# A streaming encoder step on TensorE: 1092 token columns in blocks of 512, 512 and 68 in place of three of 364

## The chip, the cores and the metric

The kernel runs on one core of a Trainium2 chip. The metric is the device time of one execution in microseconds (us); smaller is better. The core has TensorE (PE, matrix products, with its weight loads shown apart as PEld), VectorE (DVE), ScalarE (ACT), GpSimd (POOL) and SyncE (SP, here the queue of the weight transfers).

## The reference

A two-layer encoder trunk takes one inference step for two groups that share all weights: 1024 frames of a new stream and 64 frames of a running one. All sizes below are float32.

```
x = x + mixer_l(rmsnorm(x)); x = x + conv_ffn(rmsnorm(x))          # l = 0, 1; then a last rmsnorm
layer 0's mixer: proj = h @ ab_w_in (1024 x 5648); a Mamba-2 scan and a gated short convolution;
                 concat(1024, 1024) @ ab_w_out
layer 1's mixer: proj = h @ lru_w_in (1024 x 2048); convolution, gates (4 heads, 256 x 256), linear scan;
                 (gelu(gate) * hs) @ lru_w_out
conv_ffn:        g, u = h @ ffn_w_in (1024 x 5632); (gelu(conv3(g)) * u) @ ffn_w_out (2816 x 1024)
```

The outputs are the final frames and the new states of the convolutions and scans.

## The kernel before, in words

Activations lie transposed: a tile is [128 features, T token columns], T = 1092: 1024 frames of the new stream, 4 columns of padding, 64 frames of the running one. D = 1024 features are 8 such tiles (KT).

Nearly all the arithmetic is in large products of weights with these tiles. To keep float32's precision, each operand is split into two parts of type float32r, a high part h and a rest l; `weights` (lines 122 to 134) loads 128 x 512 weights from HBM through SP's queue, ScalarE rounds them to wh (line 131) and VectorE makes the rest wl (line 132). A product is then wh with xh, wl with xh and wh with xl.

`product` (lines 160 to 169) fills one PSUM tile: for every 128-row tile of the contraction and each of the three pairs, it walks over the NB = 3 blocks of BL = 364 columns. A PSUM tile (`psum`, [128, 3, 512]) has three banks of 512 columns, and each block of 364 begins at the first column of its own bank. Two such tiles are in turn. Each matmul on TensorE is preceded by a load of its 128 x 128 weights, also where the weights are those of the matmul before.

Three routines call it. `project` (lines 176 to 182) makes one tile of an input projection, 8 x 3 x 3 = 72 matmuls. `chunk` (lines 255 to 262) adds two k-tiles of an output projection to the 8 residual tiles, 18 matmuls each, and VectorE adds the PSUM tile to the residual at line 260. `part` inside `gates` makes the RG-LRU gates. The results are read from PSUM as [128, 3, 364] by VectorE (lines 260, 608, 615 and others) or ScalarE; `b3` (lines 49 to 51) gives an SBUF tile the same three-block view. dt's product at line 327 has weights of only 48 columns (w_dt).

In layer 0 the small float32 products of the scan (lines 376, 465, 480, 507, 518, 520) are generators in the list `between`; `tick` lets one advance after each k-tile of a large product, so they stand in TensorE's queue between the large matmuls. Line 520 multiplies the state st, 128 columns of weights, by 64 columns; line 480 has 128 columns; lines 376 and 465 are transposes. The program's order on each engine is then set by a scheduler when the program is built. Norms (`rms`, line 210) and the last output product (`finish`, lines 743 to 758) have their own loops over blocks of 364. The final norm at line 758 is a plain float32 product with a matrix of ones.

Of the kernel before, what the change touches and what calls it, by code (L numbers as in the profile page):

```python
# [14 lines left out]
D = 1024  # L15
# [15 lines left out]
def columns():  # L31
    """Where each small parameter stands in the packed array of them."""
    at, n = {}, 0
    for k in ("mix0", "mix1", "fn0", "fn1", "fin", "ssdn"):
        at[k] = n
        n += KT
    for k, (c, w) in CONVS.items():
        at[k + "_w"], at[k + "_b"], at[k + "_h"] = n, n + c * w, n + c * (w + 1)
        n += c * (2 * w)
    for k, c in (("ba", 8), ("bx", 8), ("lam", 8), ("st", 8), ("dsk", 8), ("dtb", 1), ("alog", 1)):  # L40
        at[k] = n
        n += c
    return at, n
# [5 lines left out]
def b3(t):  # L49
    """A [128, T] tile seen as its token blocks."""  # L50
    return t[:, 0:T].rearrange("p (b n) -> p b n", b=NB)


def program(nc, tc, a, ctx):
# [44 lines left out]

    # ---- constants and small parameters  # L100
    par = const.tile([P, NPAR], F, name="par")
# [18 lines left out]

    # ---- helpers
    def weights(src):
        """A [128, 1024] tile of weights as its halves' parts (h, l), h + l the weights."""
        out = []
        for i in range(2):
            n = n_of["w"] = n_of.get("w", 0) + 1
            raw = wp.tile([P, 512], F, tag="raw", bufs=3, name=f"raw{n}")
            h = wp.tile([P, 512], R, tag="wh", bufs=6, name=f"wh{n}")
            l = wp.tile([P, 512], R, tag="wl", bufs=6, name=f"wl{n}")
            nc.sync.dma_start(raw, src[:, i * 512:(i + 1) * 512])  # L130
            S.activation(h, raw, AF.Copy)  # L131
            V.tensor_sub(l, raw, h.bitcast(F))  # L132
            out.append((h, l))
        return out

    def piece(w, j):
        """The j-th 128 columns of a tile of weights."""
        at = slice(j % 4 * P, (j % 4 + 1) * P)
        return w[j // 4][0][:, at], w[j // 4][1][:, at]

    # small products and what follows from them, made between the parts of the large ones
    between, ticks = [], {"n": 0}
# [17 lines left out]
    def product(ps, terms):  # L160
        """ps[m, t] = the sum over terms ((wh, wl) [k, m], (xh, xl) [k, t])."""
        n = len(terms) * 3
        i = 0
        for (wh, wl), (xh, xl) in terms:
            for w, x in ((wh, xh), (wl, xh), (wh, xl)):
                for b in range(NB):
                    TE.matmul(ps[:, b, 0:BL], w, x[:, b * BL:(b + 1) * BL], start=i == 0, stop=i == n - 1)  # L167
                i += 1
            tick()
# [6 lines left out]
    def project(key, xs):  # L176
        if key not in ahead:
            prefetch(key)
        w = ahead.pop(key)
        ps = psum()  # L180
        product(ps, [(piece(w, k), xs[k]) for k in range(KT)])
        return ps[:, :, 0:BL]

# [20 lines left out]
    def rms(ss, width):  # L204
        """ss [128, T] becomes 1/sqrt(mean + eps) of its sums over the partitions, in every row."""
        v, r, out = wk(), wk(), ss
        for b in range(NB):
            at = slice(b * BL, (b + 1) * BL)
            ps = aux().rearrange("p a b -> p (a b)")[:, 0:BL]
            TE.matmul(ps, ones, ss[:, at], start=True, stop=True)  # L210
            rstd(ps, v[:, at], r[:, at], out[:, at], width)
        return out

    def rstd(sums, v, r, out, width):
        """1/sqrt(sums/width + eps): by the table, then a step of Newton's."""
        S.activation(r, sums, AF.Abs_reciprocal_sqrt, bias=eps, scale=1.0 / width)
        V.tensor_scalar(v, sums, 1.0 / width, EPS, op0=OP.mult, op1=OP.add)
        S.activation(out, r, AF.Square)
        V.scalar_tensor_tensor(out, out, -0.5, v, op0=OP.mult, op1=OP.mult)
        V.scalar_tensor_tensor(out, out, 1.5, r, op0=OP.add, op1=OP.mult)  # L220

    def history(cb, kind, i):
        """The conv buffer's columns in front of each sequence."""
        n = CONVS[kind][1] - 1
        G.memset(cb[:, 0:PAD], 0.0)
        G.tensor_copy(cb[:, PAD + S0 - n:PAD + S0], col(kind + "_h", i * n, n))  # L226
# [11 lines left out]
    def softplus(x, tmp1, tmp2):  # L238
        """In place; x may be any AP."""
        S.activation(tmp1, x, AF.Abs)  # L240
        V.tensor_scalar_min(tmp1, tmp1, 80.0)
        S.activation(tmp2, tmp1, AF.Exp, scale=-1.0)
        # e^-|x|, corrected by what its logarithm is off
        ln = softplus.ln
        S.activation(ln, tmp2, AF.Ln)
        V.tensor_add(tmp1, tmp1, ln)
        V.tensor_scalar(tmp1, tmp1, -1.0, 1.0, op0=OP.mult, op1=OP.add)
        V.tensor_mul(tmp2, tmp2, tmp1)
        V.tensor_scalar_add(tmp1, tmp2, 1.0)
        S.activation(ln, tmp1, AF.Ln)  # L250
        V.scalar_tensor_tensor(tmp1, tmp1, -1.0, tmp2, op0=OP.add, op1=OP.subtract)
        V.tensor_sub(ln, ln, tmp1)
        V.scalar_tensor_tensor(x, x, 0.0, ln, op0=OP.max, op1=OP.add)

    def chunk(xs, ws, XR, done=None):
        """XR[m] += the product of the k-tiles xs with their rows of the output weights."""
        for m in range(KT):
            ps = psum()
            product(ps, [(piece(w, m), x) for w, x in zip(ws, xs)])
            V.tensor_add(b3(XR[m]), b3(XR[m]), ps[:, :, 0:BL])  # L260
            if done:
                done(m)

    class Next:
        """The norm that follows a residual sum: its operands and row of 1/rms."""

# [14 lines left out]
    def chunks(n, produce, w_out, XR, done, after):  # L281
        """The output product over n k-tiles, two at a time, one tile behind their making."""
        tiles = {}
# [17 lines left out]

    # ---- layer 0's mixer: the norm of x
    w_in = "ab_in"
    xin, XGs = [], []
    for k in range(KT):
# [4 lines left out]
        if k == 0:  # L310
            # dt's weights: their h for the rows from 0 and their l for those from 32
            raw_dt = wp.tile([P, 512], F, tag="raw", bufs=3, name="raw_dt")[:, 0:3 * H * KT].rearrange("p (k n) -> p k n", k=KT)
# [11 lines left out]
    for k in range(KT):  # L324
        for i in range(2):
            for b in range(NB):
                TE.matmul(ps[0:3 * H, b, 0:BL], w_dt[:, k], XGs[k][i][:, b * BL:(b + 1) * BL], start=k + i == 0, stop=k + i == KT)  # L327
    dt16 = ring()
    S.activation(b3(dt16)[0:H], ps[0:H, :, 0:BL], AF.Copy)
    V.tensor_add(b3(dt16)[0:H], b3(dt16)[0:H], ps[32:32 + H, :, 0:BL])  # L330
    raw_z = wk()
# [4 lines left out]

    # dt, the running sums of dt * A in each chunk, and what follows from them
    at_d = scratch("at_d", [H, T])
# [25 lines left out]
    nc.gpsimd.dma_start(cd, al_d.partition_broadcast(P))  # L364
    # the same by token: [token of the chunk, chunk, head]
    at_t = small([P, NCH + 1, H], "at_t")
# [20 lines left out]
    def silu_conv(i, ps, make):  # L387
        """The tile i of x, B or C: scaled, through its conv and SiLU."""
        cb = conv_buffer()
# [39 lines left out]
    def heads(i, xs, zz):  # L429
        """The scan of heads 2i and 2i+1; xs and zz are [head, p] by token."""  # L430
        h0 = 2 * i
# [15 lines left out]

        # the masked decays from token to token
        for h, Rt in ((h0, Ra), (h0 + 1, Rb)):
# [7 lines left out]
        S.activation(Re, Re, AF.Exp)  # L457
        # x * dt by token, and that decayed to the chunk's end
        Xd, Xe = ring(cols=L), ring(cols=L)
# [13 lines left out]
        yield  # L473
        # the chunks' states
        Hs = ring(cols=L)
# [22 lines left out]
        yield  # L498
        # y: within the chunk, D * x, and from the state at its start
        for q in range(3):  # L500
# [75 lines left out]

    # both halves' output product
    XR, RS2 = [], {}
# [46 lines left out]

    # ---- layer 1's mixer
    XGs = nxt.xs
# [38 lines left out]
    def gates(hd, xb, sx, nx):  # L666
        ax = weights(a["lru_ax"][hd])

        def part(o):
            ps = psum()  # L670
            product(ps, [(piece(ax, 4 * k + o), sx[k]) for k in range(2)])
            return ps[:, :, 0:BL]

# [54 lines left out]
    def finish(xs, ws):  # L728
        """The last part of the output product, the final norm and y, by blocks of tokens."""
        ss = slot("ss", 2)  # L730
# [62 lines left out]

# ---- layouts
def tiles_of(w):
    """[1024, m * 128] weights as m tiles [128, k * 128]: [k in the tile, (k tile, m in the tile)]."""
    m = w.shape[1] // P
# [3 lines left out]
def by_partition(v):  # L801
    """(..., c * 128) -> [128, c, ...]."""
    v = np.asarray(v)
# [105 lines left out]
```

## Time and profile before

| what | us |
|---|---|
| median of two runs | 2793.74 (2792.61 to 2794.87) |
| span of the profiled execution, first to last instruction | 2790.8 |
| TensorE busy: matmuls, weight loads | 2745.5, 2717.2 |
| VectorE, ScalarE, GpSimd busy | 1601.7, 803.4, 242.8 |

The page lists no time of the profiled execution beyond its span. The median is 2.9 us above that. Matmuls are pipelined: a recorded duration holds the way through the array, so two in a row overlap, and the pace of a stretch is the distance of starts. The granted clock is TensorE's: 1.00 is 2.4 GHz, 0.50 is 1.2 GHz.

### The profile page before, as it was taken

The numbers are of one execution on the slowest core, as the hardware profiler recorded it, in microseconds if no ns is written. First come the engines' busy times: TensorE is split into PE (matmuls) and PEld (weight loads), VectorE is DVE, ScalarE is ACT, GpSimd is POOL, SyncE is SP. The second block draws the span as 40 slices with busy tenths as digits, with TensorE's granted clock in tenths as the row PEclk, the third lists the DMA queues.
The fourth block names the chain that finished last, engine by engine and source line by source line (L and its number), as shares of the span: only waits on it lengthen the run. The fifth ranks groups of instructions, "written<-read, shape, count | busy, mean of one in ns | idle before, by whom it ended". The sixth has DMA issues, their size and how long they took to land.

```text
span 2790.8 us, 39161 instructions
## 1 busy us (share of the span) xinstructions
PE 2745.5 (98%) x16642; PEld 2717.2 (97%) x16642; DVE 1601.7 (57%) x1723; ACT 803.4 (29%) x1083; POOL 242.8 (9%) x524
## 2 busy tenths in 40 slices
PE   8999999999999999999999999999999999999998
PEld 8999999999989999999999989999899999999997
DVE  7655665568675444444444587786744444444446
ACT  7323322232132222212212245551412112212223
POOL 1101111010030000000000030020300000000003
PEclk9999999999999999999999999999999999999999
DMA  3222332244211111111111121151111111111111
GB/s 131 78 82 81 99 97 82 86 127 138 66 43 41 46 46 46 42 46 42 46 46 45 64 82 58 55 199 53 38 46 46 42 46 45 42 46 42 42 47 68
DMA packets 83103, 183.02 MB, mean 66 GB/s; under 512 B 9808, under 2 KB 12416, under 8 KB 82928
## 3 DMA queue, kind: packets, MB, share of 16 engines
q1 hardware_dynamic: 67248, 123.40, 14.5%
q0 software_dynamic: 15392, 56.69, 6.1%
q8 instruction: 131, 2.15, 0.3%
q10 hardware_dynamic: 288, 0.42, 0.0%
q14 instruction: 44, 0.36, 0.0%
HBM read 156.81 MB, written 23.66 MB: 65 GB/s over the span
## 4 chain that ended last, share of the span: by engine, by line
PE 94%; DVE 3%; issue 1%; ACT 1%; DMA 0%; POOL 0%; SPq 0%; DVEq 0%; ACTq 0%; POOLq 0%
PE pm L167 90%; DVE xg L193 1%; PE pa L507 1%; DVE xr L260 1%; PE pa L480 1%; PE pm L743 1%; DVE xg L772 0%; PE pa L518 0%; DVE wl L132 0%; PE pm L327 0%; PE pa L210 0%; PE pa L465 0%; DMA xr<-x 0%; DMA o_keep_lru<-keep_lru 0%; ACT xg L747 0%
## 5 line engine op out<-in xcount | busy, mean ns | idle before, releaser
L167 PE MATMUL pm<-xg,wh 128*128 128x364 f32 x7104 | 1406.8, 330 | 0.0
L167 PEld LDWEIGHTS pm<-xg,wh 128*128 128x128 f32 x7104 | 1204.6, 188 | 5.8 <-issue 2.6
L167 PE MATMUL pm<-xg,wl 128*128 128x364 f32 x3552 | 783.7, 328 | 0.0
L131 ACT ACTIVATE wh<-raw 128x512 fp32r<-128x512 f32 x440 | 274.8, 628 | 1481.7 <-PE pm L167 1259.8
L167 PE MATMUL pm<-ring,wh 128*128 128x364 f32 x3360 | 662.6, 331 | 22.3 <-DVE xr L260 17.2
L167 PEld LDWEIGHTS pm<-xg,wl 128*128 128x128 f32 x3552 | 619.9, 188 | 1.1
L167 PEld LDWEIGHTS pm<-ring,wh 128*128 128x128 f32 x3360 | 573.5, 189 | 27.4 <-DVE xr L260 20.2
L260 DVE TENSOR_TENSOR xr<-xr,pm 128x1092 f32<-128x1092 f32 x264 | 340.2, 1290 | 210.2 <-PE pm L167 204.4
L132 DVE TENSOR_TENSOR wl<-raw,wh 128x512 fp32r<-128x512 f32 x440 | 310.5, 708 | 243.8 <-ACT wh L131 243.6
L167 PE MATMUL pm<-ring,wl 128*128 128x364 f32 x1680 | 373.7, 331 | 0.0
L167 PEld LDWEIGHTS pm<-ring,wl 128*128 128x128 f32 x1680 | 295.4, 189 | 0.1
L226 POOL COPY wk<-par 128x2 f32<-128x2 f32 (+1 forms) x72 | 40.0, 555 | 1709.8 <-DVE wk L608 1416.2
L236 DVE SCALAR_TENSOR_TENSOR wk<-wk,par,wk 128x1092 f32<-128x1092 f32 x104 | 140.8, 1354 | 63.3 <-ACT wk L234 61.8
L608 DVE TENSOR_TENSOR wk<-pm,ss 128x1092 f32<-128x1092 f32 x44 | 57.0, 1295 | 193.0 <-PE pm L167 192.8
L615 DVE TENSOR_TENSOR wk<-pm,wk 128x1092 f32<-128x1092 f32 x44 | 57.0, 1295 | 119.7 <-PE pm L167 119.7
L187 DVE TENSOR_TENSOR ring<-wk,ring 128x1092 fp32r<-128x1092 f32 x68 | 87.9, 1294 | 36.5 <-ACT ring L186 32.8
L186 ACT ACTIVATE ring<-wk 128x1092 fp32r<-128x1092 f32 x68 | 75.7, 1116 | 100.0 <-PE pm L167 65.4
L612 DVE TENSOR_TENSOR wk<-wk,ss 128x1092 f32<-128x1092 f32 x44 | 57.0, 1296 | 52.1 <-ACT wk L611 52.1
L234 ACT ACTIVATE wk<-wk,par 128x1092 f32<-128x1092 f32 x52 | 67.7, 1302 | 65.5 <-POOL wk L226 65.3
L611 ACT ACTIVATE wk<-wk 128x1092 f32<-128x1092 f32 x44 | 49.2, 1118 | 121.2 <-DVE wk L236 121.2
L202 POOL TENSOR_TENSOR ss<-ss,wk 128x1092 f32<-128x1092 f32 x21 | 64.7, 3082 | 172.5 <-ACT wk L201 172.0
L193 DVE SCALAR_TENSOR_TENSOR xg<-xr,par,xg 128x1092 fp32r<-128x1092 f32 x32 | 64.5, 2024 | 11.8 <-ACT xg L192 11.5
(239 smaller groups left out, 1326.4 us busy)
## 6 DMA issues: line engine op xcount, KB each, us to landing
raw<-f_in SPq DMA_DIRECT2D x176, 256.0 KB, 2.6
raw<-ab_in SPq DMA_DIRECT2D x88, 256.0 KB, 2.7
raw<-f_out SPq DMA_DIRECT2D x88, 256.0 KB, 2.6
ring<-at_d POOLq DMA_DIRECT2D x16, 546.0 KB, 6.0
raw<-ab_out SPq DMA_DIRECT2D x32, 256.0 KB, 2.7
raw<-lru_in SPq DMA_DIRECT2D x32, 256.0 KB, 2.6
xr<-x SPq DMA_DIRECT2D x8, 546.0 KB, 7.3
ring<-at_d POOLq DMA_DIRECT2D x16, 273.0 KB, 7.9
```

The lines of the kernel that those rows point to most:

```text
L131: S.activation(h, raw, AF.Copy)
L132: V.tensor_sub(l, raw, h.bitcast(F))
L167: TE.matmul(ps[:, b, 0:BL], w, x[:, b * BL:(b + 1) * BL], start=i == 0, stop=i == n - 1)
L186: S.activation(h, src, AF.Copy)
L187: V.tensor_sub(l, src, h.bitcast(F))
L193: split_last[0] = V.scalar_tensor_tensor(l, src, scale, h.bitcast(F), op0=OP.mult, op1=OP.subtract).ins
L202: by.tensor_add(ss, ss, sq)
L234: S.activation(out, cb[:, at:at + T], AF.Identity, bias=col(kind + "_b", i), scale=col(kind + "_w", i * w))
L236: V.scalar_tensor_tensor(out, cb[:, at + k:at + k + T], col(kind + "_w", i * w + k), out, op0=OP.mult, op1=OP.add)
L260: V.tensor_add(b3(XR[m]), b3(XR[m]), ps[:, :, 0:BL])
L608: V.tensor_mul(b3(cb[:, PAD:]), ps, b3(RS))
L612: V.tensor_mul(g, g, RS)
```

## The change

The 1092 columns of a large product are cut at multiples of 512, so the PSUM tile is filled as one row of 1092 columns across its three banks: 512 columns in the first, 512 in the second, 68 in the third. `flat` gives that view and is used wherever such a tile is read; `b3` becomes the plain [128, 1092] view. The dt product at line 327 is cut in the same way. The loops of `rms` and `finish` stay at 364. Comments and document strings are left out in the changed file, so lines shift by up to ten: 167 becomes 177, 520 becomes 530.

```diff
 def b3(t):
-    return t[:, 0:T].rearrange("p (b n) -> p b n", b=NB)
+    return t[:, 0:T]
+
+BANK = 512
+BLOCKS = [slice(c, min(c + BANK, T)) for c in range(0, T, BANK)]
+
+def flat(ps):
+    return ps.rearrange("p b n -> p (b n)")[:, 0:T]
...
     def product(ps, terms):
...
             for w, x in ((wh, xh), (wl, xh), (wh, xl)):
-                for b in range(NB):
-                    TE.matmul(ps[:, b, 0:BL], w, x[:, b * BL:(b + 1) * BL], start=i == 0, stop=i == n - 1)
+                for at in BLOCKS:
+                    TE.matmul(flat(ps)[:, at], w, x[:, at], start=i == 0, stop=i == n - 1)
...
     def project(key, xs):
...
-        return ps[:, :, 0:BL]
+        return flat(ps)
...
     def chunk(xs, ws, XR, done=None):
...
-            V.tensor_add(b3(XR[m]), b3(XR[m]), ps[:, :, 0:BL])
+            V.tensor_add(b3(XR[m]), b3(XR[m]), flat(ps))
...
     ps = psum()
     for k in range(KT):
         for i in range(2):
-            for b in range(NB):
-                TE.matmul(ps[0:3 * H, b, 0:BL], w_dt[:, k], XGs[k][i][:, b * BL:(b + 1) * BL], start=k + i == 0, stop=k + i == KT)
+            for at in BLOCKS:
+                TE.matmul(flat(ps)[0:3 * H, at], w_dt[:, k], XGs[k][i][:, at], start=k + i == 0, stop=k + i == KT)
     dt16 = ring()
-    S.activation(b3(dt16)[0:H], ps[0:H, :, 0:BL], AF.Copy)
-    V.tensor_add(b3(dt16)[0:H], b3(dt16)[0:H], ps[32:32 + H, :, 0:BL])
+    S.activation(b3(dt16)[0:H], flat(ps)[0:H], AF.Copy)
+    V.tensor_add(b3(dt16)[0:H], b3(dt16)[0:H], flat(ps)[32:32 + H])
...
         def part(o):
...
-            return ps[:, :, 0:BL]
+            return flat(ps)
```

TensorE's queue in layer 0, at the end of one projection (PSUM tile pm_1219), a small product of the scan (line 520, into pa) and the start of the next projection (pm_1326); xg are parts of the normed input, wh and wl parts of the weights. Before:

```order
L167 MATMUL pm_1219<-xg_152,wh_1214 128x364 x3
L167 MATMUL pm_1219<-xg_152,wl_1215 128x364 x3
L167 MATMUL pm_1219<-xg_153,wh_1214 128x364 x3
L520 MATMUL pa_1307<-xr_563,st_769 128x64
L167 MATMUL pm_1326<-xg_93,wh_1315 128x364 x3
L167 MATMUL pm_1326<-xg_93,wl_1316 128x364 x3
```

The same place in the changed kernel:

```order
L177 MATMUL pm_1219<-xg_152,wh_1214 128x512 x2
L177 MATMUL pm_1219<-xg_152,wh_1214 128x68
L177 MATMUL pm_1219<-xg_152,wl_1215 128x512 x2
L177 MATMUL pm_1219<-xg_152,wl_1215 128x68
L177 MATMUL pm_1219<-xg_153,wh_1214 128x512 x2
L177 MATMUL pm_1219<-xg_153,wh_1214 128x68
L530 MATMUL pa_1307<-xr_563,st_769 128x64
L177 MATMUL pm_1326<-xg_93,wh_1315 128x512 x2
L177 MATMUL pm_1326<-xg_93,wh_1315 128x68
L177 MATMUL pm_1326<-xg_93,wl_1316 128x512 x2
L177 MATMUL pm_1326<-xg_93,wl_1316 128x68
```

The products keep their places; each row of three blocks becomes a row of two and a row of one, and the last of each three, before the weights change, is now the short one. In the feed-forward part the same queue reads as follows at the end of a piece of the output product (pm_10740, from the parts ring of the hidden tiles) and the start of the next projection (pm_10772). Before:

```order
L167 MATMUL pm_10740<-ring_10384,wh_10595 128x364 x3
L167 MATMUL pm_10740<-ring_10384,wl_10596 128x364 x3
L167 MATMUL pm_10740<-ring_10385,wh_10595 128x364 x3
L167 MATMUL pm_10772<-xg_7005,wh_10761 128x364 x3
L167 MATMUL pm_10772<-xg_7005,wl_10762 128x364 x3
```

After:

```order
L177 MATMUL pm_10740<-ring_10384,wh_10595 128x512 x2
L177 MATMUL pm_10740<-ring_10384,wh_10595 128x68
L177 MATMUL pm_10740<-ring_10384,wl_10596 128x512 x2
L177 MATMUL pm_10740<-ring_10384,wl_10596 128x68
L177 MATMUL pm_10740<-ring_10385,wh_10595 128x512 x2
L177 MATMUL pm_10740<-ring_10385,wh_10595 128x68
L177 MATMUL pm_10772<-xg_7005,wh_10761 128x512 x2
L177 MATMUL pm_10772<-xg_7005,wh_10761 128x68
L177 MATMUL pm_10772<-xg_7005,wl_10762 128x512 x2
```

Here too nothing but the cut of each three differs. SP's queue has the same order in both kernels; on VectorE, ScalarE and GpSimd some neighbouring instructions change places.

## Rows read from the trace of the kernel before

**Rows 1.** The page: span, busy time of each engine, granted clock in 40 slices
```profile
span 2790.8 us, 39161 instructions
...
PE 2745.5 (98%) x16642; PEld 2717.2 (97%) x16642; DVE 1601.7 (57%) x1723; ACT 803.4 (29%) x1083; POOL 242.8 (9%) x524
...
PEclk9999999999999999999999999999999999999999
```

**Rows 2.** The chain that ended last: by line, and its two longest pieces
```profile
PE pm L167 90%; DVE xg L193 1%; PE pa L507 1%; DVE xr L260 1%; PE pa L480 1%; PE pm L743 1%; DVE xg L772 0%; PE pa L518 0%; DVE wl L132 0%; PE pm L327 0%; PE pa L210 0%; PE pa L465 0%; DMA xr<-x 0%; DMA o_keep_lru<-keep_lru 0%; ACT xg L747 0%
...
837.19 762.97 PE pm L167 x4585
...
1993.04 753.60 PE pm L167 x4523
```

**Rows 3.** Groups of line 167 (busy us, mean ns of one | idle before)
```profile
L167 PE MATMUL pm<-xg,wh 128*128 128x364 f32 x7104 | 1406.8, 330 | 0.0
L167 PEld LDWEIGHTS pm<-xg,wh 128*128 128x128 f32 x7104 | 1204.6, 188 | 5.8 <-issue 2.6
L167 PE MATMUL pm<-xg,wl 128*128 128x364 f32 x3552 | 783.7, 328 | 0.0
...
L167 PE MATMUL pm<-ring,wh 128*128 128x364 f32 x3360 | 662.6, 331 | 22.3 <-DVE xr L260 17.2
...
L167 PE MATMUL pm<-ring,wl 128*128 128x364 f32 x1680 | 373.7, 331 | 0.0
```

**Rows 4.** Timeline, feed-forward of layer 0 (start us, us in all, engine, line)
```profile
1100.59 1.02 PEld L167 LDWEIGHTS pm<-xg,wh 128*128 128x128 f32 x6
1100.75 1.16 PE L167 MATMUL pm<-xg,wh 128*128 128x364 f32 x6
```

**Rows 5.** Timeline of PE from 1619.4 us, at granted clock 0.50
```profile
1620.37 2.02 PE L167 MATMUL pm<-ring,wh 128*128 128x364 f32 x6
1622.18 1.11 PE L167 MATMUL pm<-ring,wl 128*128 128x364 f32 x3
```

**Rows 6.** The stretch of rows 5: us, busy us of PE, PEld, DVE, ACT, POOL; PEclk, DMA share, GB/s
```profile
1618.00:1622.00 4.00, 3.62 (x12) 3.62 (x13) 3.18 (x4) 3.64 (x4) 2.39 (x3) 0.50 0.53 212
```

**Rows 7.** The final norm's float32 products: timeline of PE, and the line's durations
```profile
2772.06 5.06 PE L758 MATMUL pa<-xg,ones 128*128 128x364 f32 x16
...
L758 PE MATMUL pa<-xg,ones x16: 469/469/469, 2772.1 to 2776.6; 128*128 128x364 f32 x16
```

**Rows 8.** Line 327's weight loads, 48 columns (ns min/median/max, first and last start)
```profile
L327 PEld LDWEIGHTS pm<-xg,w_dt x48: 120/121/201, 9.0 to 24.8; 128*48 128x48 f32 x48
```

**Rows 9.** Timeline around line 520, from 141.36 us
```profile
141.16 0.32 PE L167 MATMUL pm<-xg,wh 128*128 128x364 f32 x1
141.32 0.33 PE L520 MATMUL pa<-xr,st 128*128 128x64 f32 x2
141.33 0.19 PEld L520 LDWEIGHTS pa<-xr,st 128*128 128x128 f32 x1
141.44 0.30 PEld L167 LDWEIGHTS pm<-xg,wh 128*128 128x128 f32 x2
```

**Rows 10.** Line 480, 128 columns between loads of 128: timeline, durations
```profile
110.51 1.05 PE L480 MATMUL pa<-ring,xr 128*128 128x128 f32 x8
...
L480 PE MATMUL pa<-ring,xr x128: 270/275/275, 110.5 to 606.3; 128*128 128x128 f32 x128
```

**Rows 11.** Timeline of PEld: line 376's transposes, and what follows
```profile
82.32 0.57 PEld L376 LDWEIGHTS pa<-idm,ring 16*128 16x128 f32 x8 [0.23 <-DVE wk L390]
82.82 0.11 PEld L377 LDWEIGHTS pa<-idm,ring 16*64 16x64 f32 x1
```

**Rows 12.** What PE waited for (us in total, times, longest us)
```profile
PE pm L167 <- DVE xr L260: 17.2, 9, 4.0
```

**Rows 13.** Groups of VectorE: a read from PSUM, and one from SBUF alone
```profile
L608 DVE TENSOR_TENSOR wk<-pm,ss 128x1092 f32<-128x1092 f32 x44 | 57.0, 1295 | 193.0 <-PE pm L167 192.8
...
L612 DVE TENSOR_TENSOR wk<-wk,ss 128x1092 f32<-128x1092 f32 x44 | 57.0, 1296 | 52.1 <-ACT wk L611 52.1
```

## The prediction

> **What bounds the kernel now.** I read the page's busy times and clock first, then the chain that ended last, then the groups of line 167, then the timeline. TensorE is busy for 98% of the span, its weight loads for 97%, VectorE for 57%, and the granted clock is at its upper level nearly throughout [rows 1]. The chain shows the same: nine tenths of the span are matmuls of line 167, in pieces of thousands with no wait between them [rows 2]. So a nanosecond on each of these matmuls is paid in full, and time saved or lost on VectorE, ScalarE or the queues is not.
>
> The reader should then find the pace, not the duration. A matmul of 364 columns is recorded with 330 ns and its weight load with 188 ns [rows 3], but they are pipelined. The long pieces give the pace: (762.97 - 0.33) / 4584 = 166.4 ns for one matmul, and 166.6 ns in the second piece [rows 2]. I take 166.5, so one product of a weight piece with all 1092 columns (three matmuls) takes 499.4 ns. There is one load per matmul, although three in a row use the same weights [rows 3], and in the timeline a load begins as the matmul ahead of it begins: at 1100.59 six loads start one after the other, and at 1100.75, one pace later, the six matmuls that use them [rows 4]. So one load is under way beside one matmul, and it is free as long as the matmul is the longer of the two.
>
> **The change part by part.** Line 167 runs 7104 + 3552 + 3360 + 1680 = 15696 times [rows 3]. That is 5232 triples. Columns, loads and matmuls stay the same in number. What changes is that each triple is now 512 + 512 + 68.
>
> *A block of 512.* No row has one in this format. One end is the present pace plus 148 more columns at one per cycle of 2.4 GHz: 166.5 + 61.7 = 228.2 ns. The other end is that the pace is proportional: 166.5 x 512 / 364 = 234.2 ns. Which is nearer? At the lower clock level (1.2 GHz, granted 0.50) six matmuls take from 1620.37 to 1622.18, 302 ns each, and 364 / 1.2 is 303: a column per cycle [rows 5, 6]. At 2.4 GHz that would be 151.7, and 166.5 is measured. The plain float32 matmuls of line 758, which take two cycles for a column, keep a pace of (5.06 - 0.47) / 15 = 306 ns, only 2.7 over 728 / 2.4 [rows 7]. So the fixed part seems small and the excess of 14.8 seems to belong to fast streaming. I take 232 ns, near the proportional end. The load of 128 columns is hidden beside either.
>
> *A block of 68.* Streaming it takes about 166.5 x 68 / 364 = 31 ns. The load of the next weights can start only when this block starts. What does a load take? With 48 columns it is recorded with 121 ns [rows 8], with 128 columns 188 [rows 3], so 0.84 ns for each column and 107 ns for 128. The nearest rows in the trace are the two halves of the float32 product of line 520, each a matmul of only 64 columns between loads of 128: the second load of line 520 starts at 141.33, the load for line 167 at 141.44, and the next one at 141.44 + 0.30 - 0.19 = 141.55 [rows 9]. Two steps of 110 ns, though 64 columns stream in about half of that (line 480's 128 columns go at 111 ns each, (1.05 - 0.275) / 7) [rows 10]. The same rows show that the load does not run further ahead: line 520's second load waited for the first matmul of line 520 to begin, although a matmul of 364 columns had been running for 0.16 us. So I take 110 ns for a block of 68. From below the ends are 31 ns (load hidden) and 62 ns (the pace of line 376's transposes, whose loads are quicker: eight from 82.32 to 82.82) [rows 11]; from above 166.5, the pace of a whole block of 364.
>
> *The sum.* A triple becomes 232 + 232 + 110 = 574 ns in place of 499.4, 74.6 more. Times 5232 that is 390 us. Less what now waits anyway: TensorE waits 17.2 us, nine times, for the residual add of line 260 [rows 12], in the last pieces of an output product, where VectorE also makes the operands of the next norm. There a slower TensorE is partly covered; I take 8 off, between 0 and 17. The profiled execution has a span of 2790.8 us [rows 1] against a median of 2793.7, so 2.9 us lie around it, and these stay. 2790.8 + 390 - 8 + 2.9 = 3176 us, 13.7% more.
>
> *Edits that I cost at nothing.* VectorE and ScalarE now read PSUM as one run of 1092 columns over three banks, not three strips of 364. A read from PSUM takes 1295 ns today and one from SBUF with the same columns 1296 [rows 13], so the strips cost nothing that could be saved. Were such a read 10% slower, it would stay beside TensorE, with VectorE at 57%. The 16 triples for dt have loads of 48 columns, about 40 ns, and run in the first 25 us beside waits for data. SP's queue of weight transfers keeps its order; some neighbours change places on the other engines, which wait for TensorE as before.
>
> *A rule weighed here.* The load's cost decides the case. The Trainium skill ("TensorE: Matmul & The Clock Gate", Weight-path perf modes) says that weight loads of 128 columns in a type other than FP32 run in a fast mode, measured at about half the time. By it this block would take some 62 ns and not 110. The 0.84 ns for each column, from 121 against 188, speak against that mode here.
>
> **The rivals.**
> Fast loads: if a load for line 167 takes half, a block of 68 is paced at 62 ns as in [rows 11]; 2 x 232 + 62 - 499.4 = 26.6, times 5232 = 139, less 8: 2925 us. For it: quick loads exist in the trace. Against it: [rows 8, 9], the last of which holds a load for line 167 itself. Chance 5%.
>
> Full blocks at full rate: the 14.8 ns of excess come from the odd block size and vanish with blocks as large as a bank. 512 columns take 213.3 + 2.7 = 216 ns; 2 x 216 + 110 - 499.4 = 42.6, 223 us in all, less 8: 3009 us. For it: [rows 5, 6, 7] reach a rate without excess. Against it: today's three blocks each begin at a bank's first column already (line 167) and still show the excess. Chance 6%. The Trainium skill ("TensorE: Matmul & The Clock Gate", Back-to-back issue gap) would come out here too, with columns / 2.4 plus about 2.5 ns for a matmul; by it today's pace would be 154 ns, and the trace shows 166.5.
>
> Not slower: the load behind the short block is hidden after all, because the array keeps weights that stay the same for three matmuls, or takes the load for the next weights during the second 512. Then only columns count: 1092 at today's pace is again 499.4 ns and the time 2794 us; with full rate as well 2 x 216 + 31 - 499.4 = -36.4, so 2603 us. The point that decides is whether the load after the block of 68 can begin before that block begins. For it: two of three loads repeat the weights. Against it: the load that waited in [rows 9], and as many loads as matmuls in [rows 3]. Chance 4%, of which 1% for faster.
>
> Two passes: a short block is run like a float32 product, as two matmuls with two loads, as line 520 is. Then 220 ns, 2 x 232 + 220 - 499.4 = 184.6, 966 us: about 3750 us. Against it: nothing in the program asks for it. Chance 3%.
>
> Lower clock: the array now pauses in every triple, and the granted clock could fall to its lower level. At 1.2 GHz a triple takes at least 1092 / 1.2 = 910 ns; 410.6 x 5232 = 2148 us more, about 4940. Against it: the clock's row reads 9 in every slice, also in the first quarter, where the scan's short products stand between the large ones [rows 1]. Chance 1%.
>
> **How the numbers follow.** The forecast, loads laid bare behind each short block, has 81%. Its own range, with 5 ns either way on the 110 (the timeline's stamps have steps of 10), goes from 2 x 228.2 + 105 - 499.4 = 62 (324 us, less 17: 3101) to 2 x 234.2 + 115 - 499.4 = 84 (440 us: 3234). Taking in the case of full rate makes it 3000 to 3250; outside lie fast loads, not slower, two passes and the lower clock, with 13% together. Slower by over 2%, about what a measurement of this kernel can tell from no change: 81 + 5 + 6 + 3 + 1 = 96%; within 2%: 3%; faster: 1%.
>
> **What would show it.** In the profile after: loads in the steady stretches start 232, 232 and 110 ns apart, the 110 between the load after a block of 68 and the one before it; the pieces of the chain take 191 ns for each matmul on average, not 166.5; the reads of PSUM stay at 1295 ns; VectorE's share falls to about 51% at the same busy time; the clock stays at 1.00. The prediction is wrong if a matmul of 68 columns is followed by the next after 31 to 60 ns, if blocks of 512 come at 216, if the short blocks are recorded twice, or if the clock row shows half levels inside the long pieces.

## The result and the profile after

The changed kernel takes 3178.03 us (3177.38 and 3178.67) against 2793.74 before: a ratio of 1.138, with a 95% interval of 1.1345 to 1.1411. It is slower by 384 us, and the forecast was 3176.

The page of the changed kernel, its span, busy times and clock (to be read beside [rows 1]):

```profile
span 3176.4 us, 39156 instructions
...
PE 3139.2 (99%) x16642; PEld 2655.0 (84%) x16642; DVE 1597.5 (50%) x1723; ACT 805.4 (25%) x1083; POOL 235.2 (7%) x524
...
PEclk9999999999999999999999999999999999999999
```

TensorE is still busy all the time, with the same number of matmuls and loads. VectorE and ScalarE do the same work in a longer span, so their shares fall. The weight loads, which were busy for 97%, now show gaps: behind the short block a load runs without a matmul beside it, and beside the long blocks there is time when no load runs. The busy share of PE alone would not have told this, since a matmul that waits for its weights is recorded as busy, as the timeline below shows.

The chain that ended last, its two longest pieces (start, us, count; [rows 2] before):

```profile
942.92 879.69 PE pm L177 x4588
...
2265.00 867.12 PE pm L177 x4525
```

867.12 / 4525 is 191.6 ns for a matmul, 575 for a triple; before, 753.60 / 4523 gave 166.6 and 500. The groups of line 177, kept apart by shape:

```profile
L177 PE MATMUL pm<-xg,wh 128*128 128x512 f32 x4736 | 1538.1, 434 | 0.7 <-ACT xr L688 0.7
L177 PEld LDWEIGHTS pm<-xg,wh 128*128 128x128 f32 x7104 | 1154.8, 189 | 211.7 <-issue 2.8
L177 PE MATMUL pm<-xg,wh 128*128 128x68 f32 x2368 | 460.4, 194 | 0.0
...
L618 DVE TENSOR_TENSOR wk<-pm,ss 128x1092 f32<-128x1092 f32 x44 | 57.0, 1296 | 231.0 <-PE pm L177 230.8
```

A load still takes 189 ns, and the loads were idle for 211.7 us beside this group, where they had been idle for 5.8 [rows 3]. The short block is recorded once, not twice. The read from PSUM in one run takes 1296 ns, against 1295 in three strips [rows 13].

The steps themselves, from two narrow windows of the loads' timeline (a load starts once the matmul ahead of it has started, and in line 177 never sooner than 0.11 us after the load ahead of it; so its distance to the next is what the matmul ahead of it costs):

```profile
1200.10 0.30 PEld L177 LDWEIGHTS pm<-ring,wh 128*128 128x128 f32 x2
...
1200.44 0.54 PEld L177 LDWEIGHTS pm<-ring,wh 128*128 128x128 f32 x3
```

The first row's second load begins at 1200.10 + 0.30 - 0.19 = 1200.21, the next row's at 1200.44, and its third at 1200.44 + 0.54 - 0.19 = 1200.79. So the steps are 0.11, 0.23, and then 0.35 for two, which is 0.23 and again 0.11. That is the forecast's 232, 232 and 110. Over all of line 177 at a granted clock of 1.00, the mean steps in the trace are 108.3 behind the short block, 234.9 behind the first long one and 232.0 behind the second, 575 in all.

The matmuls' own records need care here. Around the same place, from narrow windows of the timeline:

```profile
1199.87 0.39 PE L177 MATMUL pm<-ring,wl 128*128 128x512 f32 x1
...
1200.13 0.47 PE L177 MATMUL pm<-ring,wh 128*128 128x512 f32 x1
...
1200.44 0.43 PE L177 MATMUL pm<-ring,wh 128*128 128x512 f32 x2
1200.68 0.19 PEld L177 LDWEIGHTS pm<-ring,wh 128*128 128x128 f32 x1
...
1200.71 0.70 PE L177 MATMUL pm<-ring,wh 128*128 128x512 f32 x2
```

The third row ends with a short block, which begins at 1200.44 + 0.43 - 0.19 = 1200.68, together with the load for the long block behind it. That long block is recorded as beginning at 1200.71, 0.03 us later, while its load has only just begun. Such a block is recorded with 0.47 us where the other long block has 0.39: the wait for the weights lies inside its record.

What TensorE waited for (us in total, times, longest; [rows 12]):

```profile
PE pm L177 <- DVE xr L270: 10.2, 3, 3.4
PE pm L337 <- DVE w_dt L326: 8.6, 1, 8.6
```

The residual add held it up for 17.2 us before and for 10.2 now.

One place of the changed kernel already parts two readings of the short block. dt's product has short blocks too, with loads of 48 columns, and its matmuls stand between those of the large products. The timeline of the loads there:

```profile
22.55 0.19 PEld L177 LDWEIGHTS pm<-xg,wh 128*128 128x128 f32 x1
22.66 0.17 PEld L337 LDWEIGHTS pm<-xg,w_dt 128*48 128x48 f32 x2
...
22.70 0.12 PEld L337 LDWEIGHTS pm<-xg,w_dt 128*48 128x48 f32 x1
```

The load at 22.55 has 128 columns and stands behind a short block: the next comes 0.11 us later. The load at 22.66 has 48 columns and stands behind a short block of line 177: the next comes 0.04 us later. Both short blocks stream 68 columns; behind them stands a load of 128 columns in one case and of 48 in the other (their own weights differ too, the other way round: 48 columns and 128).

### The profile page after: what moved, and what is told of

Read it like the earlier page. It is cut to its first block, busy times and chain, and to the rows that moved or that the text cites. A ratio compares the mean times of both kernels' runs of the same rounds, so it can differ in the third digit from the quotient of the medians.

```text
span 3176.4 us, 39156 instructions
## 1 busy us (share of the span) xinstructions
PE 3139.2 (99%) x16642; PEld 2655.0 (84%) x16642; DVE 1597.5 (50%) x1723; ACT 805.4 (25%) x1083; POOL 235.2 (7%) x524
## 4 chain that ended last, share of the span: by engine, by line
PE 96%; DVE 2%; ACT 1%; issue 1%; DMA 0%; POOL 0%; DVEq 0%; ACTq 0%; POOLq 0%
PE pm L177 92%; DVE xg L203 1%; PE pa L517 1%; PE pa L490 0%; PE pm L753 0%; PE pa L528 0%; DVE xg L782 0%; DVE xr L270 0%; PE pm L337 0%; PE pa L220 0%; DVE wl L142 0%; PE pa L475 0%; DMA par<-par 0%; DMA wk<-yz_d 0%; DMA o_keep_lru<-keep_lru 0%
## 5 line engine op out<-in xcount | busy, mean ns | idle before, releaser
L177 PE MATMUL pm<-xg,wh 128*128 128x512 f32 (+1 forms) x7104 | 1581.1, 354 | 0.7 <-ACT xr L688 0.7
L177 PEld LDWEIGHTS pm<-xg,wh 128*128 128x128 f32 x7104 | 1154.8, 189 | 211.7 <-issue 2.8
L177 PE MATMUL pm<-xg,wl 128*128 128x512 f32 (+1 forms) x3552 | 875.1, 354 | 0.0
L177 PE MATMUL pm<-ring,wh 128*128 128x512 f32 (+1 forms) x3360 | 747.8, 356 | 14.0 <-DVE xr L270 10.2
L177 PEld LDWEIGHTS pm<-xg,wl 128*128 128x128 f32 x3552 | 577.1, 189 | 103.0
L177 PEld LDWEIGHTS pm<-ring,wh 128*128 128x128 f32 x3360 | 550.5, 190 | 115.4 <-DVE xr L270 11.2
L177 PE MATMUL pm<-ring,wl 128*128 128x512 f32 x1680 | 416.2, 356 | 0.0
L177 PEld LDWEIGHTS pm<-ring,wl 128*128 128x128 f32 x1680 | 275.3, 191 | 49.6
L618 DVE TENSOR_TENSOR wk<-pm,ss 128x1092 f32<-128x1092 f32 x44 | 57.0, 1296 | 231.0 <-PE pm L177 230.8
L625 DVE TENSOR_TENSOR wk<-pm,wk 128x1092 f32<-128x1092 f32 x44 | 57.0, 1295 | 197.2 <-PE pm L177 197.2
L197 DVE TENSOR_TENSOR ring<-wk,ring 128x1092 fp32r<-128x1092 f32 x68 | 88.0, 1295 | 35.5 <-ACT ring L196 33.6
L622 DVE TENSOR_TENSOR wk<-wk,ss 128x1092 f32<-128x1092 f32 x44 | 57.0, 1296 | 52.1 <-ACT wk L621 52.1
L203 DVE SCALAR_TENSOR_TENSOR xg<-xr,par,xg 128x1092 fp32r<-128x1092 f32 x32 | 55.3, 1736 | 17.0 <-ACT xg L202 17.0
```

The lines of the kernel that those rows point to most:

```text
L177: TE.matmul(flat(ps)[:, at], w, x[:, at], start=i == 0, stop=i == n - 1)
L197: V.tensor_sub(l, src, h.bitcast(F))
L203: split_last[0] = V.scalar_tensor_tensor(l, src, scale, h.bitcast(F), op0=OP.mult, op1=OP.subtract).ins
L618: V.tensor_mul(b3(cb[:, PAD:]), ps, b3(RS))
L622: V.tensor_mul(g, g, RS)
```

## The experiments

The theory: a load of 128 weight columns takes 108 ns, cannot begin before the matmul ahead of it, and lies bare where that matmul streams for less; columns stream at 0.456 ns each (233 / 512, 166 / 364). The rivals: a price of the short block itself (a fixed extra, or slow streaming under some size), a load that is paid only when weights change, and a price of the flat reading or of blocks that fill a bank.

**The short block made longer, in three steps, and then taken away.** The first block ends at the end of the first bank, the second fills the second bank, and the third begins the third bank, so that the flat view stays in one piece (FIRST is 452, 388, 340 and 290 in c128, c192, c240 and c290, named by the last block):

```diff
-BLOCKS = [slice(c, min(c + BANK, T)) for c in range(0, T, BANK)]
+FIRST = 452
+BLOCKS = [slice(0, FIRST), slice(FIRST, FIRST + BANK), slice(FIRST + BANK, T)]
...
-    return ps.rearrange("p b n -> p (b n)")[:, 0:T]
+    return ps.rearrange("p b n -> p (b n)")[:, BANK - FIRST:BANK - FIRST + T]
```

> Blocks of 452, 512 and 128, read flat as in the changed kernel. Theory (a load of 128 weight columns takes 108 ns and lies bare behind a block that streams for less; columns stream at 0.456 ns each): 206 + 233 + 108 = 548 ns a triple against 575 in the changed kernel, so 27 x 5232 = 143 us less, 3035 us; steps of loads 206, 233 and 108. Rival one (a short block costs a fixed extra of some 76 ns whatever its size): 3178. Rival two (a block under 256 columns streams in four passes): 128 columns take 213 ns, a triple 652, about 3580 us.

> Blocks of 388, 512 and 192. Theory: 192 columns stream in 88 ns, still less than the load's 108: 177 + 233 + 108 = 519 ns a triple, 57 x 5232 = 296 us under the changed kernel, 2882 us. Rival one (a fixed extra for a short block): 3178. Rival two (four passes under 256 columns): 320 ns for the short block, 730 a triple, about 3990 us.

> Blocks of 340, 512 and 240. Theory: 240 columns stream in 109 ns, as long as the load, so nothing lies bare: 155 + 233 + 110 = 498 ns a triple, the time of the kernel before, 2780 to 2805 us, same. Rival one (a fixed extra for any block that is shorter than the others): 3178. Rival two (four passes under 256 columns): 400 ns for the short block, about 4400 us. Rival three (part of the loss lies in the flat reading or in blocks that fill a bank, not in the short block): well above 2805, and c290 with it.

> Blocks of 290, 512 and 290, with the flat reading over three banks kept: the change without a short block. Theory: 132 + 233 + 132 = 498 ns a triple, 2780 to 2805 us, same as before; the flat reading brings and costs nothing. Rival three (the flat reading or the full-bank block costs time of its own): above 2805 by its share. A gain from the flat reading would show as under 2780.

Measured (c128 and c192 ran once): c128 3036.6 us, c192 2940.0, c240 2855.8 (ratio to before 1.0222, 1.0205 to 1.0239), c290 2806.2 (1.004, 1.0025 to 1.0055). The last long piece of the chain of each, in this order:

```profile
2165.13 825.17 PE pm L178 x4526
```
```profile
2108.50 784.99 PE pm L178 x4527
```
```profile
2053.74 753.65 PE pm L178 x4527
```
```profile
1999.77 759.28 PE pm L178 x4523
```

For a triple that is 547, 520, 499.4 and 503.6 ns, against 575 in the changed kernel and 500 before. The expectations for the triple were 548, 519, 498 and 498. The price of the short block shrinks just as its streaming grows toward the load's 108 ns, and it is gone at 240 columns. A fixed extra would have left the first two at 3178; four passes under 256 columns would have given 652 ns at 128 columns. Both fall. The flat reading and the full bank fall as well, but for c290's 12 us: 503.6 - 500 over 5232 triples is 19 us in its pace. The steps of the loads in the trace show where it lies. c290's first block, 290 columns from column 0, takes 132.7 ns, as columns do elsewhere; the 512 columns from column 290 take 235.1, where the same block takes 231 to 232 in the other cuts made this way; and the 290 from column 802 take 135.8. These two are the only blocks in any of the cuts that begin at a column which four does not divide. No run tests whether that is the cause.

In time, though, c192 and c240 missed their expectation, by 58 us and by 51 to 76, and the long pieces don't hold these. They lie between them. c240 waits longer for the other engines, and its mean granted clock is lower, 0.989 against 0.996 before (the core's row, then the longest waits of TensorE):

```profile
core 0: 2851.5 us, clock 0.989
```
```profile
PE pm L178 <- DVE xr L271: 21.8, 10, 3.5
PE pm L338 <- DVE w_dt L327: 8.9, 1, 8.9
PE pa L221 <- DVE wk L228: 6.6, 5, 4.7
PE pm L178 <- ACT xr L689: 6.4, 4, 2.9
PE pm L178 <- ACT xr L690: 5.3, 3, 3.2
```

Of the 60.7 us that c240's span is longer than the span before, 33.3 are idle time of TensorE (span less busy time, 78.6 against 45.3 us). The lower clock stands for some 20 more, an estimate: 1.1% of c240's span against 0.4% of the span before.

The scheduler writes other queues for these kernels: in the order in which VectorE executed its some 1700 instructions in the traces (told apart by operation and tile), 141 stand elsewhere in c240 than in the kernel before and 135 in c192, but 12 in c290. So the next pair takes two cuts that differ by four columns and stand on the two sides of this.

**The same block, two orders.** c252 has blocks of 328, 512 and 252, and nearly c240's order on VectorE, ScalarE and GpSimd (9 of VectorE's instructions stand elsewhere). c256 has 324, 512 and 256, and an order as near to the kernel before as c290's (12); between c252 and c256 it is 140. The edit is FIRST = 328 and FIRST = 324 in the lines above.

> Blocks of 328, 512 and 252. In c240 the long pieces kept the pace of the kernel before, and the 60 us over it lay in more waits of TensorE for the other engines, whose queues the scheduler had written in another order. This kernel's queues have nearly c240's order on VectorE, ScalarE and GpSimd; its shortest block streams in 115 ns, 7 over the load. Theory (the 60 us are the order's, not the block's): steady pace 166.5 a matmul, total near c240's, 2840 to 2860 us. Rival (a load beside a block of about its own length costs extra): under c240 by most of the 60 us, some 2800 us.

> Blocks of 324, 512 and 256, four columns from c252, with the order of c290 and nearly of the kernel before on VectorE, ScalarE and GpSimd. Theory (the 60 us of c240 are the order's): steady pace 166.5 a matmul, 2792 to 2810 us, some 45 us under c252. Rival (a load beside a block of about its own length costs extra): within 10 us of c252.

Measured: c252 2849.4 us (1.0195, 1.0177 to 1.0213), c256 2782.4 us (0.9956, 0.994 to 0.9972). The last long piece and the longest waits of TensorE, first of c252, then of c256:

```profile
2048.89 753.76 PE pm L178 x4527
```
```profile
PE pm L178 <- DVE xr L271: 26.1, 13, 3.5
PE pm L338 <- DVE w_dt L327: 8.9, 1, 8.9
PE pa L221 <- DVE wk L228: 6.7, 5, 4.8
PE pm L178 <- ACT xr L689: 6.6, 4, 2.9
PE pm L178 <- ACT xr L690: 6.5, 4, 3.1
```
```profile
1984.21 751.58 PE pm L178 x4523
```
```profile
PE pm L178 <- DVE xr L271: 11.8, 13, 1.7
PE pm L338 <- DVE w_dt L327: 9.0, 1, 9.0
PE pm L178 <- ACT xr L689: 2.9, 1, 2.9
PE pa L221 <- DVE wk L228: 2.6, 1, 2.6
PE pm L178 <- ACT ring L197: 1.7, 1, 1.7
```

The pace is 166.5 against 166.2 ns, at most 5 us in the whole, and the times differ by 67 us, where 45 were expected; c252 lies in its range, c256 10 us under its own. The block's length near the load's is not it, for c252's block is longer than c240's by twelve columns and the time hardly changed. What else differs is the order in which VectorE and ScalarE do their work beside TensorE. TensorE is idle for 85.4 us in c252 and for 41.9 in c256, and the mean granted clock is 0.992 against 0.997, some 14 us by the same kind of estimate. I did not run one cut with both orders, so that the order alone makes the 67 us stays argued. Besides it, the two programs differ by the four columns and, mostly in the first 60 us, in TensorE's own queue, where dt's matmuls stand elsewhere among those of the first projections.

c256 also takes less time than the kernel before, by 0.4% (0.3 to 0.6): too little to count as faster at 2%, but clear of the spread of these runs. Its pace (751.58 / 4523 = 166.2 against 166.6) accounts for some 6 us of the 12.

**The short block in the middle.** The array meets the same weights three times in a row. With the order 512, 68, 512, the load behind the short block repeats weights that are there already:

```diff
 BLOCKS = [slice(c, min(c + BANK, T)) for c in range(0, T, BANK)]
+BLOCKS = [BLOCKS[0], BLOCKS[2], BLOCKS[1]]
```

> The changed kernel with the order 512, 68, 512 in each triple: behind the short block now stands a load of the same 128 weight columns that the array already holds, not of new ones. Theory (every matmul loads its weights, same or not, and the load waits for the matmul ahead to begin): the same 575 ns a triple and 3178 us, steps of 233, 108, 233. Rival (only a change of weights costs a load, or the array keeps weights that repeat): the short block takes 31 ns, 77 x 5232 = 403 us less, 2775 us.

Measured, in one run: 3176.8 us. The last long piece of its chain:

```profile
2264.50 865.82 PE pm L178 x4525
```

191.3 ns for a matmul, as in the changed kernel. A load of weights that the array holds costs as much as one of new weights, and it is not hidden in a long block that lies further ahead.

**A smaller load behind the same block.** Here the first block of 512 in all but the first and last pass of each product uses 48 of the 128 weight columns, which leaves the other 80 output rows of that block without these terms:

```diff
                 for at in BLOCKS:
-                    TE.matmul(flat(ps)[:, at], w, x[:, at], start=i == 0, stop=i == n - 1)
+                    m = 48 if at.start == 0 and 0 < i < n - 1 else P
+                    TE.matmul(flat(ps)[0:m, at], w[:, 0:m], x[:, at], start=i == 0, stop=i == n - 1)
```

> The changed kernel, but the first block of 512 in all but the first and last pass of a product is computed with 48 of its 128 weight columns (the other rows of that block miss these terms), so that the load behind most short blocks has 48 columns. Streaming is the same: 22 of 24 loads in each of 148 input products and 4 of 6 in each of 280 others, 4376 in all. Theory (the load's columns set the price, 0.84 ns each): 48 columns take 40 ns, the step behind such a short block falls from 108 to 42 ns, 66 x 4376 = 289 us less, 2889 us. Rival (a short block has a floor of its own near 108 ns, or streams slowly): no change, 3178 us.

Measured, in one run: 2900.8 us. The page's span and busy times, and two groups of loads:

```profile
span 2898.6 us, 39156 instructions
...
PE 2851.7 (98%) x16642; PEld 2364.0 (82%) x16642; DVE 1598.8 (55%) x1723; ACT 803.0 (28%) x1083; POOL 235.3 (8%) x524
```
```profile
L178 PEld LDWEIGHTS pm<-xg,wh 128*128 128x128 f32 x5032 | 929.0, 189 | 121.9 <-ACT xr L689 1.7 <-issue 1.2
...
L178 PEld LDWEIGHTS pm<-xg,wh 128*48 128x48 f32 x2072 | 251.1, 121 | 88.4 <-issue 1.5
```

PE is busy for 287.5 us less than in the changed kernel (3139.2 - 2851.7) with every column still streamed; 289 were expected from the smaller loads alone. Of the 12 us by which the time missed, 9.7 are waits: the span holds 46.9 us beside PE's busy time, against 37.2 in the changed kernel. The step itself, from the loads' timeline:

```profile
1300.29 0.23 PEld L178 LDWEIGHTS pm<-xg,wl 128*48 128x48 f32 x2
```

The first load of the two has 48 columns and stands behind a short block, the second has 128 and begins at 1300.29 + 0.23 - 0.19 = 1300.33. So the step is 0.04 us, where the same block in the changed kernel is followed by 0.11. A floor of the short block itself falls.

## Why the prediction was right

**The bound.** It was read from the share of the chain and the pieces without a wait. The result bears it out: 575 - 500 = 75 ns for a triple, times 5232, is 392 us, and the span grew by 385.6.

**The block of 512.** The forecast chose 232 ns, near the proportional end of 228 to 234. With 575 for a triple and 108 for the short block, a long one took 233.5 on average. The rival of full blocks at full rate (216 ns, 3009 us) is gone: a block that fills a bank streamed at 0.453 to 0.459 ns a column, one of 364 at 0.457.

**The block of 68.** 110 ns was taken from the two halves of line 520's product [rows 9], and the timeline gives 0.11, the mean of the trace 108.3. So each long block was put some 1.5 ns too low and the short one 2 too high; that the total came within 2 us is in part luck. ld48 and dt's product show that it is the load's columns, mid that repeated weights are loaded again, c128 to c240 that the price is the load less the streaming. The Trainium skill's fast mode for weight loads ("TensorE: Matmul & The Clock Gate", Weight-path perf modes), by which the forecast put the step at some 62 ns, shows for the loads of line 177 in no run here: 128 columns took 108 ns behind the short block.

**The waits.** 8 us were taken off for waits on the residual add that a slower TensorE covers. That wait fell from 17.2 to 10.2 us, 7.0 in all. All of TensorE's idle time (span less busy time) fell from 45.3 to 37.2, by 8.1, while its busy time grew by 393.7, and 393.7 - 8.1 is the 385.6 by which the span grew. Whether the slower TensorE covers these waits or the other order of the queues avoids them, no run tells.

**The parts costed at nothing.** The reads of PSUM stayed at 1296 ns, and c256, with the flat reading and no short block, is within half a per cent of the kernel before. The order of the other engines' queues was also put at nothing, because they wait for TensorE as before. In the changed kernel, where 103 of VectorE's instructions stand elsewhere (and, mostly in the first 50 us, dt's matmuls in TensorE's own queue), that held. In c192, c240 and c252 a reordering of 135 to 141 went with 28 to 40 us more idle time of TensorE than in the kernel before. One would say that a slower TensorE covers such an order, but ld48 speaks against this as the whole reason. None of VectorE's, ScalarE's or GpSimd's instructions stands elsewhere there than in the changed kernel, and its TensorE, busy for 2851.7 us, is no slower than c192's with 2864.7; yet it is idle for 46.9 us and c192's for 73.1. So the changed kernel's order costs little even then. The forecast had no row for this, and that the scheduler wrote such an order was luck. What makes the other orders costly stays open.

**The signs.** Two of the signs that the prediction named were badly put. The step of 110 ns lies between the load behind a short block and the load after it, not the one before it. And a matmul of 68 columns is recorded with the next one beginning 31 ns later (the median in the trace), which was to show the prediction wrong. The recorded start of a matmul is not the pace: the wait for the weights stands in that next matmul's record, and the steps of the loads and the pace of the chain came as forecast.

**The clock.** It stayed at its upper level inside the long pieces (1.00 from 942 to 1822 us and from 2265 to 3132), though the array now waits in each triple.

## What to carry to other kernels

Where every matmul loads its own weights, cut the moving columns into blocks of which the shortest still streams for as long as a load: here 128 weight columns took 108 ns and a block needed about 240 columns. Fuller blocks gain nothing if the rest becomes a short one; the price is the load less the short block's streaming, once for each short block. When a cut changes, look also at whether the scheduler has rewritten the other engines' queues, and compare the pace inside the long pieces apart from the waits between them.

## What the runs showed of the hardware beyond that

At a granted clock of 1.00, float32r columns streamed at 0.453 to 0.463 ns each in blocks of 252 to 512 (c290's two odd blocks apart), some 2.2 for each nanosecond, where the lower level gave one for each cycle [rows 5, 6]. It is nearly a rate and not a price for each matmul: by the steps of the loads, 252 columns took 116.0 ns in c252, 364 took 166.5 in the kernel before and 512 took 232.0 in the changed one, which is 11.0, 14.8 and 18.7 ns over a column per cycle of 2.4 GHz. What sets it stays open.
